# Hard-max attention on one core: dots grouped by four tiles, three GpSimd drains in the loop, and a reordered serial tail

## The chip, the core and the metric

The kernel runs on one core of one Trainium2 chip. The metric is the device time of one execution in microseconds (us); lower is better. A profile of one execution accompanies each kernel. Engines are named as in the profile: PE (TensorE matmul), PEld (its weight loads), DVE (VectorE), ACT (ScalarE), POOL (GpSimd), SP (the queue of SyncE).

## The reference

```python
B, Sq, Sk, D = 4, 4096, 4096, 128        # q, k, v: float32
logits = np.matmul(q, k.transpose(0, 2, 1))
best = np.argmax(logits, axis=-1)
return v[b_idx, best, :]                 # one row of v for each query
```

No softmax and no weighted sum: only the winning key's value row is needed.

## The kernel before

The queries are cut into 128 tiles of 128 rows. For each tile:

1. PE scores groups of four keys, with sums and differences of keys; ACT evicts with Abs or Relu, DVE folds what is left (`W`) and takes the eight highest groups with one MAX8 (`TOP`).
2. GpSimd gathers, by an indirect DMA per tile, the three key differences of the best group (`kg`). DVE computes three dots per row with them (product, two halvings, a reduction), and `pick` selects the winner within the group.
3. GpSimd gathers the value rows (`vr`), one indirect DMA per tile, and SP stores them.
4. Rows whose winner is in doubt are collected. The second half's are rechecked in a serial tail: gathers `FR`, `FQ`, three `FK`, exact dots, a last value gather `FV`, and a scatter into the output. A branch (`all_rows`) guards a fallback over everything.

The program order on each engine is fixed by a small scheduler that runs when the kernel is built. An iteration `it` places the instructions of a tile; the key gathers wait in `near_q`, the value gathers in `late_q`, and `issue` hands out a few of each per iteration:

```python
def dots(c, x, m):
    ...
    # start 2 iterations (1 in the last 24) after the key gathers are issued
    yield "until", lambda: ("kg", x) in done, 1 if x >= TAIL else 2
    nc.vector.tensor_tensor(out=prod, in0=kg, in1=..., op=OP.mult)          # m = 2 tiles
    yield "dve",
    nc.vector.tensor_tensor(out=p1, in0=prod[..., 0:64], in1=prod[..., 64:128], op=OP.add)
    yield "dve",
    nc.vector.tensor_tensor(out=p2, in0=p1[..., 0:32], in1=p1[..., 32:64], op=OP.add)
    yield "dve",
    nc.vector.tensor_reduce(out=d[:, x - c0:x - c0 + m, 1:4], in_=p2, ...)

def issue(it):
    ...
    while near_q and (n < 1 + (it >= T - 28 and len(near_q) > 2) or near_q[0] in marks):
        g = near_q.pop(0)
        n += g not in marks
        g()
    ...
    take_late(2 if n == 0 and len(late_q) > 4 or it >= T - 24 and it % 2 == 0 else 1)

def flags_last(...):                      # the serial tail, cut
    late(LATE)                            # 8 value gathers
    get(FR, ...); get(FQ, ...); late(1)
    ...
    get(FK[:, 0:3], ...)                  # three gathers
    late(3)
    win = whole(exact(FK, FQ, gb, 3, "fe"))
    get(FV, v_flat, win, B * Sk)
    late(1 << 20)
    ...
    all_rows()                            # loads the count of hard rows, branches
    nc.gpsimd.indirect_dma_start(out=out_flat, ..., in_=FV, ...)
```

A `mark` stands in `near_q` behind the gathers of a group; when it is popped, the group's dots get their place.

## Time and profile before

| | |
|---|---|
| median of the runs | 466.7 us (466.5 to 467.3) |
| span of the profiled execution | 465.5 us, mean granted PE clock 0.949 |
| last MAX8 starts | 420.1 us; 45.5 us of serial tail follow |
| final GpSimd drain | 454.19 to 464.68 us |

The page's first part gives busy time, share of the span and instructions of each engine. Its second part gives the busy tenths of an engine in 40 equal slices of the span. Of the kernel before:

```profile
PE 380.2 (82%) x1834; PEld 168.3 (36%) x1834; DVE 417.8 (90%) x825; ACT 376.8 (81%) x437; POOL 318.1 (68%) x345
...
DVE  2689999999999999999999999999998999998330
...
POOL 8233557877677888776678876677777777767730
```

DVE looks like the limit and POOL, with 68%, like an engine with room. Here is POOL's timeline of the kernel before, in the middle of the span (start, duration, engine, line, operation, output and input; in brackets the idle time before it and what ended that):

```profile
197.14 1.01 POOL L304 DMA_INDIRECT vr<-in_v_dram,win  x1 [0.30 <-issue]
198.45 0.95 POOL L250 DMA_INDIRECT kg<-k,cand  x1 [0.30 <-issue]
199.70 1.01 POOL L304 DMA_INDIRECT vr<-in_v_dram,win  x1 [0.30 <-issue]
201.01 0.94 POOL L250 DMA_INDIRECT kg<-k,cand  x1 [0.30 <-issue]
...
206.39 0.94 POOL L250 DMA_INDIRECT kg<-k,cand  x1 [0.57 <-DVE p L269]
```

Each gather occupies POOL for about 1.0 us and is followed by 0.30 us in which POOL is idle but waits for nothing ("issue"). A gather therefore costs 1.25 to 1.31 us of POOL's time.

The tail, in POOL's timeline of the kernel before, and the drains of the program's last line:

```profile
444.37 1.00 POOL L304 DMA_INDIRECT vr<-in_v_dram,win  x1 [0.30 <-issue]
447.55 1.00 POOL L498 DMA_INDIRECT FV<-in_v_dram,xw_fe  x1 [2.19 <-DVE hi L573]
454.42 1.03 POOL L534 DMA_INDIRECT out_dram<-FV,rowk_e  x1 [5.87 <-issue]
```

```profile
L806 POOLq DRAIN  x3: 46/109/10489, 454.2 to 465.2; - x3
```

The second fence is the view of one source line: the least, median and greatest duration in ns of three records. The long drain is placed ahead of the scatter's own time because POOL's sequencer reaches it while the scatter is still queued: it ends at 464.68 us, 9.2 us after the scatter's issue ended (455.45).

### The profile page before, as it was taken

Reading aid. Unit: us, or ns where it says so; the run is one execution under the profiler, and the core shown is the slowest. Engines: PE = TensorE matmul, PEld = TensorE weight load, DVE = VectorE, ACT = ScalarE, POOL = GpSimd, SP = SyncE. Lnnn points to the kernel's source line nnn. Section 1 sums busy time; section 2 is a strip of 40 time slices with the busy share of each in tenths; the row PEclk is TensorE's granted clock in tenths of the full one; section 3 lists DMA queues with packets and bytes.
Section 4 is the critical chain, followed back from the end, with each engine's and each line's share of the span. In section 5 each row is a group of like instructions: output and inputs, shape, how many; then the busy total and the mean of one; then the engine's idle time right before and its main releaser. Section 6 shows DMA issues by size and latency. Waiting matters only on the chain.

```text
span 465.5 us, 6396 instructions
## 1 busy us (share of the span) xinstructions
PE 380.2 (82%) x1834; PEld 168.3 (36%) x1834; DVE 417.8 (90%) x825; ACT 376.8 (81%) x437; POOL 318.1 (68%) x345
## 2 busy tenths in 40 slices
PE   8999999998999889999998889998998888850100
PEld 4444444443444344444443334443333333320000
DVE  2689999999999999999999999999998999998330
ACT  2999999999999989999997889999998888840000
POOL 8233557877677888776678876677777777767730
PEclk9999999999999999999999999999999999995555
DMA  7934576853325877943235653423432333322320
GB/s 130 227 66 96 107 103 97 139 120 85 80 76 135 148 140 128 121 126 81 79 98 137 129 116 94 100 80 87 110 101 79 86 86 99 87 71 68 94 74 4
DMA packets 43624, 47.54 MB, mean 102 GB/s; under 512 B 25000, under 2 KB 33451, under 8 KB 43584
## 3 DMA queue, kind: packets, MB, share of 16 engines
q0 software_dynamic: 18752, 30.97, 33.7%
q1 hardware_dynamic: 24832, 16.13, 13.1%
q8 instruction: 14, 0.23, 0.2%
q14 instruction: 26, 0.21, 0.2%
HBM read 39.59 MB, written 12.19 MB: 111 GB/s over the span
## 4 chain that ended last, share of the span: by engine, by line
DVE 31%; issue 23%; ACT 13%; PE 13%; DMA 9%; POOL 7%; POOLq 0%; DVEq 0%; ACTq 0%
DVE W L228 14%; ACT A L202 10%; PE psn L193 5%; DVE TOP L232 5%; PE psn L212 4%; DMA kg<-k,cand 4%; ACT E L215 4%; DMA vr<-in_v_dram,win 3%; DVE prod L265 3%; PE pd L193 3%; POOL kg L250 3%; POOL vr L304 2%; DVE D L274 2%; DVE p L269 2%; DMA natk<-in_k_dram 2%
## 5 line engine op out<-in xcount | busy, mean ns | idle before, releaser
L202 ACT ACTIVATE A<-pd 128x1024 f16<-128x1024 f32 x256 | 258.6, 1041 | 23.0 <-PE pd L193 22.7
L250 POOL DMA_INDIRECT kg<-k,cand x128 | 127.4, 995 | 85.1 <-issue 26.6
L228 DVE SCALAR_TENSOR_TENSOR W<-psn,E 128x1024 int16<-128x1024 f32 x128 | 166.0, 1297 | 7.0 <-ACT E L215 5.5
L193 PE MATMUL pd<-kT,qT 128*128 128x512 f16 x512 | 151.8, 378 | 15.7 <-ACT A L202 14.8
L193 PE MATMUL psn<-kT,qT 128*128 128x512 f16 x512 | 151.8, 378 | 15.3 <-ACT A L202 7.9
L304 POOL DMA_INDIRECT vr<-in_v_dram,win x128 | 136.6, 1067 | 39.0 <-issue 37.5
L193 PEld LDWEIGHTS <-qT 128*128 128x128 f16 x1024 | 98.4, 97 | 163.9 <-issue 76.0
L232 DVE MAX8 TOP<-W 128x8 f32<-128x1024 f32 x128 | 155.8, 1217 | 0.0
L212 PE MATMUL psn<-A,identh 128*128 128x512 f16 x512 | 152.1, 378 | 0.0
L215 ACT ACTIVATE E<-psn 128x1024 int16<-128x1024 f32 x128 | 132.2, 1033 | 5.0 <-PE psn L212 5.0
L212 PEld LDWEIGHTS <-identh 128*128 128x128 f16 x512 | 49.6, 97 | 60.8
L265 DVE TENSOR_TENSOR prod<-kg,natq 128x768 f16<-128x768 f16 x64 | 34.9, 546 | 3.9 <-DMA kg<-k,cand 3.9
L269 DVE TENSOR_TENSOR p<-prod 128x384 f16<-128x384 f16 x64 | 22.3, 349 | 0.1
L274 DVE TENSOR_REDUCE D<-p 128x6 f32<-128x192 f16 x64 | 21.5, 336 | 0.1
L173 ACT ACTIVATE kT<-uk 128x256 f16<-128x256 f32 x48 | 20.1, 419 | 0.9 <-PE uk L170 0.9
L64 POOL DMA_DIRECT2D natk<-in_k_dram x27 | 16.1, 599 | 0.9 <-POOLq L795 0.8
L67 POOL DMA_DIRECT2D natq<-in_q_dram x27 | 16.3, 605 | 0.2
L169 PE MATMUL uk<-identh,natk 128*128 128x128 f16 x96 | 15.8, 218 | 0.6 <-ACT A L202 0.6
L272 DVE TENSOR_TENSOR p<-p 128x192 f16<-128x192 f16 x64 | 15.7, 245 | 0.0
L464 PE MATMUL fp_e<-n_e,tri 128*128 128x1 f32 x2 | 0.6, 361 | 16.7 <-DVE n_e L462 16.7
L170 PEld LDWEIGHTS <-natk 128*128 128x128 f16 x96 | 9.3, 97 | 7.7 <-issue 5.3
L169 PEld LDWEIGHTS <-natk 128*128 128x128 f16 x96 | 9.3, 97 | 5.6
(147 smaller groups left out, 133.5 us busy)
## 6 DMA issues: line engine op xcount, KB each, us to landing
out_dram<-vr SPq DMA_DIRECT2D x32, 256.0 KB, 2.2
natq<-in_q_dram POOLq DMA_DIRECT2D x26, 128.0 KB, 3.2
k<-kd SPq DMA_DIRECT2D x8, 384.0 KB, 4.2
natk<-in_k_dram POOLq DMA_DIRECT2D x24, 128.0 KB, 3.9
kg<-k,cand POOLq DMA_INDIRECT x128, 2.8
vr<-in_v_dram,win POOLq DMA_INDIRECT x128, 2.8
natq<-in_q_dram POOLq DMA_DIRECT2D x1, 768.0 KB
natk<-in_k_dram POOLq DMA_DIRECT2D x1, 512.0 KB, 5.2
```

What stands on the lines that cost most here:

```text
L169: nc.tensor.matmul(out=o, lhsT=natk[b % 2][:, h, 4 * m + x, :], rhs=identh, start=True, stop=False)
L193: nc.tensor.matmul(out=ps[:, n * 512:(n + 1) * 512], lhsT=qT[b % 2][:, qt * P:(qt + 1) * P], rhs=kT[b % 2][:, u * 1024 + n * 512:u * 1024 ...
L202: nc.scalar.activation(out=A, in_=ps, func=AF.Abs)
L212: nc.tensor.matmul(out=ps[:, n * 512:(n + 1) * 512], lhsT=identh, rhs=A[:, n * 512:(n + 1) * 512], start=False, stop=True)
L215: nc.scalar.activation(out=E, in_=ps, func=AF.Relu, scale=QSCALE)
L228: nc.vector.scalar_tensor_tensor(out=W_t[t % NW].bitcast(I16)[:, 1::2], in0=ps, scalar=QSCALE, in1=E, op0=OP.mult, op1=OP.max)
L232: nc.vector.max(out=TOP[:, t, :], in_=W_t[t % NW].bitcast(FP32))
L250: near_q.append(lambda j=j: nc.gpsimd.indirect_dma_start(out=kg[:, j].rearrange("p f d -> p (f d)"), out_offset=None, in_=k16[t0 // NQT], ...
L265: nc.vector.tensor_tensor(out=prod, in0=kg, in1=natq[b % 2][:, x - b * NQT:x - b * NQT + m, :].unsqueeze(2).to_broadcast([P, m, 3, P]), op ...
L269: nc.vector.tensor_tensor(out=p1, in0=prod[:, :, :, 0:64], in1=prod[:, :, :, 64:128], op=OP.add)
L274: nc.vector.tensor_reduce(out=d[:, x - c0:x - c0 + m, 1:4], in_=p2, axis=AX_X, op=OP.add)
L304: late_q.append(lambda j=j: nc.gpsimd.indirect_dma_start(out=vr[:, j, :], out_offset=None, in_=v_flat, in_offset=IOA(ap=win[:, i + j:i + j ...
```

## The change

Its intent: pay for the long final drain in pieces inside the loop; take FV's landing out of the branch's wait; shorten the last dependent steps; and save DVE's fixed cost per operation by dots over four tiles up to tile 72. The diff, cut to its core:

```diff
+DRAINS = (28, 60, 92)
-LATE = 8
+LATE = 7
@@ dots
-        yield "until", lambda: ("kg", x) in done, 1 if x >= TAIL else 2
+        yield "until", lambda: ("kg", x) in done, 2 if m < 4 and x < TAIL else 1
+        # product in halves of two tiles; p1, p2 and the reduction over all m tiles;
+        # for m = 4 these are spread over several iterations
@@ flags_last
-        late(3)
-        win = whole(exact(FK, FQ, gb, 3, "fe"))
-        get(FV, v_flat, win, B * Sk)
         late(1 << 20)
         ...
-        all_rows()
+        win = whole(exact(FK, FQ, gb, 3, "fe"))
+        all_rows(hi)
+        get(FV, v_flat, win, B * Sk)
@@ issue
-        while near_q and (n < 1 + (it >= T - 28 and len(near_q) > 2) or near_q[0] in marks):
+        if it in DRAINS:
+            nc.gpsimd.drain()
+            owed[0] += 2
+            return
+        behind = len(near_q) > (2 if it >= T - 28 else 4)
+        while near_q and (n < 1 + behind or near_q[0] in marks):
...
+        # two owed value gathers are caught up, one every third iteration
@@ gathers
+            m = 4 if t1 <= T - 56 else 2 if t < T - 2 else 1
@@ after the loop: cand and key gather of tile T-2 ahead of fold(T-1); flags_first ahead of the last two dots
```

More of the change, by code (lines that the diff above doesn't have):

```diff
@@ L21 @@
 QSCALE = 128.0
+DRAINS = (28, 60, 92)
 TAU = 8.0
 NEAR = 0.5
-LATE = 8
+LATE = 7
+NKG = 6
 @with_exitstack
@@ L245, in gather @@
                                 op0=OP.bitwise_and, op1=OP.bitwise_xor)
-        kg = rp.tile([P, n, 3, P], FP16, tag=f"kg{n}", name=f"kg_{t0}", bufs=8)
-        assert len(kg_t) < 8
+        kg = rp.tile([P, 4, 3, P], FP16, tag="kg", name=f"kg_{t0}", bufs=NKG)[:, 0:n]
+        assert len(kg_t) < NKG
         kg_t[t0] = kg
@@ L261, in dots @@
         b = x // NQT
-        yield "until", lambda: ("kg", x) in done, 1 if x >= TAIL else 2
+        gap = ("wait", 1) if m == 4 else ("dve",)
+        yield "until", lambda: ("kg", x) in done, 2 if m < 4 and x < TAIL else 1
         kg = kg_t.pop(x)
-        prod = rp.tile([P, m, 3, P], FP16, tag=f"prod{m}", name=f"prod_{x}")
-        nc.vector.tensor_tensor(out=prod, in0=kg, in1=natq[b % 2][:, x - b * NQT:x - b * NQT + m, :].unsqueeze(2).to_broadcast([P, m, 3, P]),
-                                op=OP.mult)
-        yield "dve",
-        p1 = rp.tile([P, m, 3, 64], FP16, tag=f"p1{m}", name=f"p1_{x}")
+        prod = rp.tile([P, 4, 3, P], FP16, tag="prod", name=f"prod_{x}")[:, 0:m]
+        h = min(m, 2)
+        for i in range(0, m, h):
+            nc.vector.tensor_tensor(out=prod[:, i:i + h], in0=kg[:, i:i + h],
+                                    in1=natq[b % 2][:, x + i - b * NQT:x + i + h - b * NQT, :].unsqueeze(2).to_broadcast([P, h, 3, P]),
+                                    op=OP.mult)
+            yield gap
+        p1 = rp.tile([P, 4, 3, 64], FP16, tag="p1", name=f"p1_{x}")[:, 0:m]
         nc.vector.tensor_tensor(out=p1, in0=prod[:, :, :, 0:64], in1=prod[:, :, :, 64:128], op=OP.add)
-        yield "dve",
-        p2 = rp.tile([P, m, 3, 32], FP16, tag=f"p2{m}", name=f"p2_{x}")
+        yield gap
+        p2 = rp.tile([P, 4, 3, 32], FP16, tag="p2", name=f"p2_{x}")[:, 0:m]
         nc.vector.tensor_tensor(out=p2, in0=p1[:, :, :, 0:32], in1=p1[:, :, :, 32:64], op=OP.add)
@@ L274, in dots @@
         nc.vector.tensor_reduce(out=d[:, x - c0:x - c0 + m, 1:4], in_=p2, axis=AX_X, op=OP.add)
-        done.add(("dot", x))
+        done.update(("dot", i) for i in range(x, x + m))
     def pick(c, t0, t1):
@@ L280, in pick @@
         d = D_t[c % 4][:, 0:n, :]
-        yield "until", lambda: all(("dot", x) in done for x in range(t0, t1, 2)), 0
+        yield "until", lambda: all(("dot", x) in done for x in range(t0, t1)), 0
         cand = cand_t.pop(c)
@@ L524, in flags_last @@
             nc.vector.tensor_tensor(out=HARD, in0=HARD, in1=a, op=OP.add)
-        late(3)
-        win = whole(exact(FK, FQ, gb, 3, "fe"))
-        get(FV, v_flat, win, B * Sk)
         late(1 << 20)
+        hi = fp.tile([1, 1], mybir.dt.int32, tag="hi")
+        nc.vector.tensor_copy(out=hi, in_=HARD[0:1, :])
         ok = fp.tile([P, 1], FP32, tag="ok", name="ok_e")
@@ L557, in exact @@
         yield "dve", 0.17
-        win = fp.tile([P, 1], U32, tag="xw", name=f"xw_{name}")
+        win = fp.tile([P, 1], U32, tag=f"xw{R}", name=f"xw_{name}")
         nc.vector.tensor_reduce(out=win, in_=lt, axis=AX_X, op=OP.min)
@@ L569, in whole, with all_rows @@
                 return s.value
-    def all_rows():
-        hi = fp.tile([1, 1], mybir.dt.int32, tag="hi")
-        nc.vector.tensor_copy(out=hi, in_=HARD[0:1, :])
+    def all_rows(hi):
         left = nc.values_load(hi[0:1, 0:1], min_val=0, max_val=1 << 24,
@@ L679, in issue @@
             rest[0] = it + 3
-        take_late(2 if n == 0 and len(late_q) > 4 or it >= T - 24 and it % 2 == 0 else 1)
+        more = n == 0 and len(late_q) > 4 or it >= T - 24 and it % 2 == 0
+        if owed[0] and n < 2 and it % 3 == 0 and len(late_q) > 2:
+            owed[0] -= 1
+            more = True
+        take_late(2 if more else 1)
+    owed = [0]
     def gathers(t):
         for c, (t0, t1) in enumerate(chunks):
-            if t0 <= t < t1 and ((t - t0) % 2 or t == t1 - 1):
-                x = t0 + (t - t0) // 2 * 2
-                gather(c, x, t - x + 1)
+            m = 4 if t1 <= T - 56 else 2 if t < T - 2 else 1
+            if t0 <= t < t1 and (t - t0) % m == m - 1:
+                gather(c, t - m + 1, m)
             if t == t0:
@@ L747 @@
     top(T - 2)
+    gathers(T - 2)
+    flush()
     fold(T - 1)
     top(T - 1)
-    gathers(T - 2)
     gathers(T - 1)
@@ L771 @@
         dot = [s for s in live if s["kind"] == "dots" and s["c"] == c]
+        last = c == len(chunks) - 1
         while dot:
-            two, dot = dot[:2], dot[2:]
+            if last and len(dot) == 2:
+                flags_first(T // 2, T)
+            two, dot = (dot[:1], dot[1:]) if last else (dot[:2], dot[2:])
             drain(two)
-        last = c == len(chunks) - 1
-        if last:
-            flags_first(T // 2, T)
         drain([p], "cnt" if last else None)
```

## The prediction

> **What bounds it now.** One tile takes about 2.93 us in the middle of the span. In the timeline the VectorE starts there follow one another without a gap: start to start, fold W 1.19, MAX8 1.14, and for a pair of tiles product 0.47, two halvings 0.27 and 0.16, reduction 0.25, candidate 0.06: 5.87 us for two tiles. VectorE is busy 20.0 of 20.0 us in the windows from 40 to 100 us. ScalarE is nearly as full (19.5 to 20.0; three evictions of 0.92 start to start, plus a 0.37 us key copy in two of three tiles). The loop ends near 421 us; 44 us of serial tail follow. Its last part, in the records of the L576, L534 and L806 lines: the branch on the hard-row count is loaded at 447.6, waits for the last value gather FV to land (450.7), clears semaphores for 2.4 us, and the last scatter starts at 454.42. Then a GpSimd drain runs until 464.68, about 9.2 us after the scatter's issue ended, though the scatter landed near 456.7.
>
> **Change, piece by piece.**
> 1. Drains. GpSimd issued 324 DMAs. I take the final drain's length to grow with the DMAs since the previous drain (inferred from the edit; one long drain doesn't show it). About 85 remain after the drain in iteration 92: an estimate is 9.2 x 85/324 = 2.4 us instead of 9.2; with the scatter's landing as floor, I take 6 us off. Each drain in the loop costs GpSimd 2 to 3 us; GpSimd is 68% busy and waits for VectorE there, so most is hidden; up to 1 us of late gathers.
> 2. Branch ahead of FV. The wait for FV's landing (3.1 us after its start) leaves the branch, which now waits for an earlier gather; the chain becomes branch, FV, scatter. About 1 to 2 us.
> 3. Single-tile last gathers, tile 126's key gather before the last fold, flags ahead of the last dots. Now the last key gather starts at 423.09 and its product at 425.92. One gather (1.3 us) less in front, a shorter last dot, and 0.7 us of flag work moved ahead: 2.5 us earlier. The recheck read FR stands behind 7 value gathers instead of 8 (1.3 us each), so GpSimd passes the gain on. Together with 2: about 5 us.
> 4. Dots of four tiles for tiles 0 to 71. The product stays split in pairs, so per four tiles it saves one start each of two halvings, the reduction and the candidate: 0.05 to 0.07 us fixed part each (from 0.27 at 384 against 0.16 at 192 elements), 0.24 us, 4.3 us over 18 groups. The Trainium skill, "VectorE: DVE Perf Modes", rules for kernel authors, says to minimise the op count; the trace's fixed parts agree. But ScalarE has hardly any slack before 100 us and needs about 23.6 us for 8 tiles later against VectorE's 23.9, so only 1.5 us reaches the time.
>
> **Sum.** 6 + 5 + 1.5 - 0.5 = 12 us: 454.5 us, 8 in 10 between 450.5 and 460. Faster by over 2%: 0.74; within 2%: 0.24; slower: 0.02.
>
> **What would show it.** The last drain under 4 us; three drains of 2 to 3 us in the loop with VectorE gapless beside them; last TOP 1 to 2 us earlier; FV after the branch.
>
> **What would make it wrong.** A drain of fixed length: no gain at the end and 9 us of stalled gathers at three places. Gathers that lag after a drain, so products wait for kg. The 2.4 us clear being longer ahead of FV. ScalarE setting the pace throughout, so four-tile dots give nothing.

## The result, and the profile after

| | before | after |
|---|---|---|
| median | 466.67 us (466.47 to 467.32, 4 runs) | 477.97 us (477.23 to 478.18, 4 runs) |
| span of the profiled execution | 465.5 us | 476.4 us |
| last MAX8 starts | 420.1 us | 435.4 us |
| from there to the end | 45.5 us | 41.0 us |

The ratio is 1.0237 (95% interval 1.0219 to 1.0255): slower by 2.4%. A ratio here is the mean time of one kernel's fast runs over that of the other's of the same rounds, so it is not quite the ratio of the quoted medians.

The tail became 4.5 us shorter; the loop became 15.3 us longer. The lines of the page and of the waits (engine and line, what it waited for, us in total, times, longest) after the change:

```profile
PE 383.7 (81%) x1834; PEld 168.9 (35%) x1834; DVE 415.3 (87%) x758; ACT 377.3 (79%) x437; POOL 317.6 (67%) x345
...
DVE  2689999999999988899999999988985999889730
...
POOL 9313458747778887747778876377777777676740
```

```profile
POOL kg L252 <- issue: 48.5, 97, 7.3
...
DVE prod L270 <- DMA kg<-k,cand: 20.3, 16, 3.1
```

DVE has less work (415.3 us instead of 417.8), and no longer runs gapless. It waited 20.3 us in 16 places for key gathers; before, the same two waits were

```profile
POOL kg L250 <- issue: 26.6, 86, 0.8
...
DVE prod L265 <- DMA kg<-k,cand: 3.9, 3, 1.8
```

The drains, by the view of their source lines (three in the loop, then those of the program's end), and POOL's and DVE's timelines around the second:

```profile
L679 POOLq DRAIN  x3: 9603/10947/12037, 94.5 to 299.9; - x3
```

```profile
L823 POOLq DRAIN  x3: 46/109/10321, 465.2 to 476.1; - x3
```

```profile
199.46 1.31 POOL L252 DMA_INDIRECT kg<-k,cand  x1 [0.30 <-issue]
208.08 0.95 POOL L252 DMA_INDIRECT kg<-k,cand  x1 [7.31 <-issue]
```

```profile
209.20 1.29 DVE L230 SCALAR_TENSOR_TENSOR W<-psn,E 128x1024 int16<-128x1024 f32 x1
211.59 0.56 DVE L270 TENSOR_TENSOR prod<-kg,natq 128x768 f16<-128x768 f16 x1 [1.10 <-DMA kg<-k,cand]
```

A drain's record starts when POOL's sequencer reaches it, with about four gathers still queued in front of it on the engine. So 12.04 us of record are 6.6 us of standstill after the last gather's issue, and 7.31 us from gather to gather. And the final drain hardly got shorter: it still ends 9.05 us after the scatter's issue. The end of the tail after the change, in POOL's timeline, with FV behind the branch:

```profile
462.62 0.99 POOL L504 DMA_INDIRECT FV<-in_v_dram,xw_fe  x1 [5.10 <-DMA out_dram<-vr]
465.49 1.03 POOL L541 DMA_INDIRECT out_dram<-FV,rowk_e  x1 [1.87 <-DMA FV<-in_v_dram,xw_fe]
```

### The profile page after: what moved, and what is told of

Read it like the earlier page. It is cut to its first block, busy times and chain, and to the rows that moved or that the text cites. A ratio compares the mean times of both kernels' runs of the same rounds, so it can differ in the third digit from the quotient of the medians.

```text
span 476.4 us, 6325 instructions
## 1 busy us (share of the span) xinstructions
PE 383.7 (81%) x1834; PEld 168.9 (35%) x1834; DVE 415.3 (87%) x758; ACT 377.3 (79%) x437; POOL 317.6 (67%) x345
## 5 line engine op out<-in xcount | busy, mean ns | idle before, releaser
L310 POOL DMA_INDIRECT vr<-in_v_dram,win x128 | 134.3, 1049 | 39.0 <-issue 37.2
L270 DVE TENSOR_TENSOR prod<-kg,natq 128x768 f16<-128x768 f16 (+1 forms) x65 | 35.4, 545 | 20.4 <-DMA kg<-k,cand 20.3
L275 DVE TENSOR_TENSOR p<-prod 128x384 f16<-128x384 f16 (+2 forms) x47 | 19.9, 423 | 0.1
L280 DVE TENSOR_REDUCE D<-p 128x6 f32<-128x192 f16 (+2 forms) x47 | 19.3, 413 | 0.1
L278 DVE TENSOR_TENSOR p<-p 128x192 f16<-128x192 f16 (+2 forms) x47 | 13.5, 288 | 0.1
```

The lines of the kernel that those rows point to most:

```text
L270: nc.vector.tensor_tensor(out=prod[:, i:i + h], in0=kg[:, i:i + h], in1=natq[b % 2][:, x + i - b * NQT:x + i + h - b * NQT, :].unsqueeze(2 ...
L275: nc.vector.tensor_tensor(out=p1, in0=prod[:, :, :, 0:64], in1=prod[:, :, :, 64:128], op=OP.add)
L310: late_q.append(lambda j=j: nc.gpsimd.indirect_dma_start(out=vr[:, j, :], out_offset=None, in_=v_flat, in_offset=IOA(ap=win[:, i + j:i + j ...
```

## The experiments

### What the runs can be used for

The eighteen runs went out in seven jobs. Three of the jobs (ten runs) fell on chips where the kernel before itself took 502 to 520 us, at a mean granted clock of 0.915 to 0.936 instead of 0.945 to 0.950; in the traces of the kernels that ran beside it the clock fell to one half again and again, and the kernels' differences there mix with that. Their ratios are not used. On an undisturbed chip, the kernel before took 465 to 470 us. All main readings below are from four jobs (eight runs); the disturbed ones stand together at the end of this section. All differences between kernels below are near or under 2%; where one is called a gain or a loss, that rests on the interval of its ratio.

### How long a drain takes

For each long drain I took from POOL's records the time from the end of the last DMA issue before it to its end, and counted the DMAs issued since the previous drain (or since the program's start):

| kernel | DMAs since the last drain | us from the last issue's end |
|---|---|---|
| after, drains 1 to 3 | 61, 80, 73 | 5.06, 6.60, 6.03 |
| before with drains, 1 to 3 | 64, 78, 70 | 5.30, 6.44, 5.78 |
| after, final | 110 | 9.05 |
| before with drains, final | 112 | 9.21 |
| before, final | 324 | 9.23 |
| after without drains, final | 324 | 9.23 |

Eight drains lie on a straight line of 0.082 to 0.083 us a DMA (5.06/61, 9.21/112). The two over 324 DMAs don't: they have the length of about 112. (In the run with the look-up restored, below, 113 DMAs gave 9.29 us.) So both readings that I had held against each other were half right: the length does grow with the DMAs since the last drain, but not all the way. I call this a cap near 112; no count between 113 and 324 was measured, so whether the length stays the same in between or starts over once is not shown. The kernel before paid at its end for 112 DMAs, and not for its 324. The changed kernel pays for 61 + 80 + 73 = 214 more inside the loop, 17.7 us of POOL's time, and for 110 at the end, which saves 0.2 us.

### The drains alone, on the kernel before

```diff
 # kernel before, in issue()
+        if it in DRAINS:              # (28, 60, 92)
+            nc.gpsimd.drain()
+            owed[0] += 2
+            return
 # and the two owed value gathers, as in the change
```

> The kernel before with the three drains and their skipped iterations alone. Theory A: a drain costs GpSimd about 0.083 us for each DMA issued since the last one, at most about 112 of them (the four drains of the changed kernel, from the end of the last issue to the drain's end: 5.06, 6.60, 6.03 and 9.05 us after 61, 80, 73 and 110 DMAs; before, 9.23 after 324). So 5 to 7 us of stall each, 8 to 15 us slower than before in all, 475 to 482 us, and still about 9 us of drain at the end. Rival B: within 2 us of before.

Measured: 468.31 us against 467.00, ratio 1.0035 (1.0007 to 1.0063). The drains were as long as expected, 5.3 to 6.4 us, and yet the program lost only some 1.6 us. The expected 8 to 15 us were a miss: the stalls are real, but here they were hidden. What hid them can be counted. In POOL's DMA records I summed the idle time beyond the usual 0.30 us between one issue and the next, leaving out the gap that holds a drain:

| POOL's spare time, us, by tile | 32 to 64 | 64 to 100 | 100 to 127 |
|---|---|---|---|
| before | 3.8 | 8.7 | 3.5 |
| before with drains | 0.0 | 0.9 | 0.3 |
| after without drains, look-up at each turn (below) | 1.9 | 5.6 | 1.7 |
| the same with drains | 0.0 | 0.6 | 0.5 |
| after without drains | 2.6 | 6.6 | 5.2 |
| after | 0.0 | 2.8 | 5.4 |

The kernel before had 16.0 us to spare from tile 32 on. From gather to gather the three drains took 6.1, 7.1 and 6.6 us, and used up 14.8 us of it. POOL at "68% busy" was full afterwards.

### The changed kernel without its drains

```diff
-DRAINS = (28, 60, 92)
+DRAINS = ()
```

> A repeat of the kernel without drains: the chip of the first job ran even the kernel before at 502 to 513 us, with dips of the granted clock. Theory A: on a chip where before takes 467 us, last MAX8 near 418 us, tail near 41 us, 459 to 461 us; VectorE's wait for kg under 5 us. Rival B (four-tile dots make VectorE wait for kg): near 475.

Measured: 468.25 us against 467.00, ratio 1.0030 (1.0004 to 1.0055). The drains, with the iterations that they skip, account for 9.7 of the changed kernel's 11.3 us (477.97 - 468.25, in different jobs). But the rest of the change, from which I had expected a gain of 6 us, was no gain either. The loop was ahead of the kernel before by 4.4 us at tile 80 (MAX8 of that tile at 265.0 instead of 269.4), and then took 85.2 us from tile 104 to tile 127, where the kernel before took 76.9. The tail was 41.0 us, as in the changed kernel. DVE's waits, and its timeline where the loss begins:

```profile
DVE prod L270 <- DMA kg<-k,cand: 11.9, 6, 3.5
```

```profile
346.86 0.25 DVE L278 TENSOR_TENSOR p<-p 128x192 f16<-128x192 f16 x1
349.61 0.56 DVE L270 TENSOR_TENSOR prod<-kg,natq 128x768 f16<-128x768 f16 x1 [2.49 <-DMA kg<-k,cand]
...
352.93 0.24 DVE L278 TENSOR_TENSOR p<-p 128x192 f16<-128x192 f16 x1
356.68 0.56 DVE L270 TENSOR_TENSOR prod<-kg,natq 128x768 f16<-128x768 f16 x1 [3.51 <-DMA kg<-k,cand]
```

The order of the DMAs on POOL shows why (k a key gather, v a value gather, F one of the recheck's DMAs; the last 64 of POOL's DMAs):

```
before               vkvvkvkvvkvkvvkvkvvkFvkvkvkFvvkvkkvkvvkvkkvkkkvvvvvvvvFFvFFFvvFF
after, no drains     kvvvkkvvvkkvvvkkvvvkkvvvkkFvvvkkFvvkkvvkkvvkkvkkvvvvvvvFFvFFFvFF
```

In the changed program the two key gathers of a pair go out together. This comes from the line of the diff that looks like a mere rewriting: `behind` is computed once, ahead of the loop. In the kernel before the condition was looked up at each turn. With two gathers and a mark in `near_q` its length is 3, one gather is popped, the length is 2, and the loop stops; the second gather goes out in the next iteration. With the look-up made once, both go out at once, the mark follows in the same iteration, and the pair's dots are placed one iteration earlier. DVE then reaches the product before POOL has got to the gather, behind three value gathers in a row. The line also acts in the stage of the four-tile dots, where the limit is 4: four gathers and a mark make five, and two go out at once. In the traces of the kernels without drains, with the look-up made once and at each turn, the order of POOL's DMAs differs from the start.

### That look-up alone, in both directions

```diff
 # kernel before
-        while near_q and (n < 1 + (it >= T - 28 and len(near_q) > 2) or near_q[0] in marks):
+        behind = it >= T - 28 and len(near_q) > 2
+        while near_q and (n < 1 + behind or near_q[0] in marks):
```

> A repeat on another chip: the kernel before, with the look-up whether GpSimd is behind made once ahead of the issue loop. Theory D: 6 to 9 us slower than before, last MAX8 near 427 us instead of 420, all of it after tile 100. Rival: within 1 us of before.

Measured: 472.90 us against 466.95, ratio 1.0129 (1.0111 to 1.0147): 6 us slower by this line alone, with the last MAX8 at 425.8. The tail did not become shorter here: 46.7 us against 45.5. (The profiled execution had lost 1.2 us before tile 100 already, with a 3.4 us dip of the clock at 256 us; the rest came after.) DVE's waits for key gathers were

```profile
DVE prod L265 <- DMA kg<-k,cand: 8.4, 5, 2.5
```

And the other way round, the changed kernel without drains, with the look-up at each turn:

```diff
 # changed kernel, DRAINS = ()
-        behind = len(near_q) > (2 if it >= T - 28 else 4)
-        while near_q and (n < 1 + behind or near_q[0] in marks):
+        limit = 2 if it >= T - 28 else 4
+        while near_q and (n < 1 + (len(near_q) > limit) or near_q[0] in marks):
```

> A repeat on another chip: the last job's chip ran even the kernel before at 508 to 520 us with many dips of the granted clock, and its ratios are not used. The changed kernel without drains, with the look-up whether GpSimd is behind made at each turn. Theory D: against 468.3 without drains alone, 459 to 462 us; VectorE's wait for kg under 5 us. Rival: 468.

Measured: 463.73 us against 466.95, ratio 0.9929 (0.9911 to 0.9946). The 4.5 us between this and the run without drains (in different jobs) are the look-up's; the wait was

```profile
DVE prod L270 <- DMA kg<-k,cand: 5.1, 3, 2.9
```

It is short of the expected 459 to 462 us, because the tail grew from 41.0 to 44.3 us: with the gathers going out one by one the last dots and picks come later, and three value gathers instead of one stand between the last FK and the branch, which waits for them to land. The look-up made once had cost 6.8 us in the loop (last MAX8 at 425.6 against 418.8; 1.9 us of it by tile 80, 265.0 against 263.1) and had given back 3.3 us in the tail.

### Does restoring either one hide the drains again?

Why did the drains cost 9.7 us here and 1.6 us there? One theory (E) was the grace: the four-tile dots start one iteration after their gathers instead of two.

```diff
 # changed kernel, with its drains
-        ..., 2 if m < 4 and x < TAIL else 1
+        ..., 2 if x < TAIL else 1
```

> Second repeat: the changed kernel with its drains, a four-tile dot starts two iterations after its last key gather's issue. Theory E: 472 to 475 us, and the 5.9 us that the first two drains cost up to tile 92 shrink to under 2. Rival (GpSimd is short of time in all): 477 to 478.

Measured: 477.18 us against 466.83, ratio 1.0216 (1.0157 to 1.0274), so the rival's number. The first drain's cost did go (MAX8 of tile 48 3.1 us ahead of before, as without drains), the second's did not (tile 68 1.0 us behind, without drains 3.3 ahead). Theory E falls as the main cause. The waits only moved:

```profile
DVE prod L270 <- DMA kg<-k,cand: 17.1, 14, 4.0
```

The other was the look-up, with the drains kept:

> Second repeat: the changed kernel with its drains, the look-up at each turn as before. Theory D: the loss between tiles 92 and 127 (12.5 us against before) shrinks to 4 to 6, 470 to 472 us. If GpSimd is short of time in all: 474 to 476.

(The edit is the one above, with DRAINS as in the change.) Measured: 473.81 us against 466.83, ratio 1.0147 (1.0087 to 1.0206). About 4 us came back (from 477.97, in different jobs), the look-up's own cost, the lower end of what had been expected if POOL is short of time in all. Against the same kernel without drains the ratios give 1.0147/0.9929 = 1.022: there the drains cost 2.2%, 10 us, to some 3 us by the two intervals (the two profiled executions are 8.0 us apart), so about as much look-up or not. The table of spare time fits this only in part. Here the faster loop left POOL 9.2 us instead of 16.0, drains of about 20 us used 8.1 of it, and an estimate from these is a loss of 12 us; for the kernel before the same sum is 20 - 15 = 5, where 1.6 was measured. For the changed kernel itself it is 20 - 6 = 14, where 9.7 was measured. So the sum is 1.5 to 4 us too high. And it can be made only afterwards: the changed kernel without drains had 14.4 us to spare, nearly as much as the kernel before, but its drains used up only 6.2 of it. That POOL stands still for the drains and that DVE then waits for its gathers is shown; why the kernel before could hide so much more of this stays open.

### What the rest of the change is worth

Tail changes alone: no drains, look-up at each turn, and two-tile dots (with `NKG` back at 8 buffers for key gathers, as many as before).

```diff
 # changed kernel without drains, look-up at each turn
-            m = 4 if t1 <= T - 56 else 2 if t < T - 2 else 1
+            m = 2 if t < T - 2 else 1
```

> The changed kernel without drains, look-up at each turn, dots of two tiles throughout: the tail's changes alone. If GpSimd sets the pace from tile 32 on, the four-tile dots' lead is taken back and this comes within 1.5 us of the 463.7 us of no_drains_rule_b: 464 to 465.5 us, last MAX8 near 420, tail 44 to 44.5. Rival (the four-tile dots carry the gain): 466 to 467.

Measured: 465.97 us against 466.72, ratio 0.9984 (0.9955 to 1.0014), the same as before within its interval; the tail was 44.2 us instead of 45.5. With four-tile dots the ratio was 0.9929, so these are worth about 0.5%, 2.5 us, with intervals that nearly touch. In the two profiled executions their lead over two-tile dots was 5.3 us at tile 80 (MAX8 at 263.1 against 268.4) and 0.4 us at the last tile (418.8 against 419.1). The rest of these two loops, from tile 80 to the last MAX8, four-tile dots first (busy us of PE, PEld, DVE, ACT and POOL with the instructions, then the granted clock, the DMA share and GB/s):

```profile
263.10:418.80 155.70, 128.75 (x570) 53.58 (x568) 150.56 (x318) 128.60 (x140) 115.84 (x114) 0.99 0.34 93
268.40:419.10 150.70, 127.62 (x566) 53.37 (x565) 147.79 (x305) 127.59 (x139) 109.70 (x108) 0.99 0.33 92
```

DVE was busy there 2.8 us longer with the four-tile dots: more than half of the lead at tile 80 was work put off (dots of 74 tiles had been begun by then, against 76). The rest went into waits for key gathers, 4.2 us against 1.7 after tile 80.

### A version that beats both

In the changed kernel the pairs shorten the tail when they come at the very end, and the hope was that they cost little if they come only there:

```diff
 # changed kernel without drains
+        limit = 2 if it >= T - 28 else 4
+        pair = it >= 120 and len(near_q) > limit
+        while near_q and (n < 1 + (pair or len(near_q) > limit) or near_q[0] in marks):
```

> No drains, look-up at each turn up to iteration 119, pairs of key gathers together from 120 on, so that only one value gather instead of three stands between the last recheck gather and the branch. Tail 41 us as in no_drains_b instead of 44.3, at 1 to 3 us of waits in the last 8 tiles: 461 to 463.5 us. If the waits are worth more than the shorter tail: 464 to 466.

Measured: 462.00 us against 466.72, ratio 0.9899 (0.9869 to 0.9928): the lowest median of all kernels here, 1.0% faster than before. (Its interval overlaps that of the look-up at each turn throughout, 0.9911 to 0.9946.) POOL's timeline of its tail has one value gather ahead of the branch, the scatter is issued at 448.52, and the waits for key gathers are small:

```profile
438.26 1.00 POOL L504 DMA_INDIRECT FK<-in_k_dram,gb_e  x1 [0.31 <-issue]
439.56 1.10 POOL L310 DMA_INDIRECT vr<-in_v_dram,win  x1 [0.30 <-issue]
445.76 0.99 POOL L504 DMA_INDIRECT FV<-in_v_dram,xw_fe  x1 [5.10 <-DMA out_dram<-vr]
448.52 1.03 POOL L541 DMA_INDIRECT out_dram<-FV,rowk_e  x1 [1.76 <-DMA FV<-in_v_dram,xw_fe]
```

```profile
DVE prod L270 <- DMA kg<-k,cand: 3.4, 4, 1.2
```

The tail was 41.5 us. Its last 9 us are still the final drain.

### The runs on disturbed chips

These ten gave correct results. First job (before: 502 to 513 us): the changed kernel without drains 511.5 (ratio 1.0088), with the drains taken out but their iterations still skipped 516.8 (1.0176), the four-tile dots alone 513.5 (1.0141), the tail alone 505.1 (0.9934).

> The changed kernel without its three drains, all else kept. Theory A (the drains stop GpSimd for 5 to 7 us each, and VectorE then waits for late key gathers): the loss goes, last MAX8 near 418 us instead of 435.4, the tail stays near 41 us, total about 459 to 461 us; VectorE's wait for kg falls from 20.3 us to under 5; the final drain stays at about 9 us after the last scatter. Rival B (four-tile dots, with one iteration of grace instead of two, make VectorE wait for kg): the wait stays near 20 us and the total near 475.

> The changed kernel with the drain instructions taken out, but the three iterations still skip their gathers and the two owed gathers are caught up. Theory A: as without drains, within 1 us, 459 to 462 us. Rival C (the skipped iteration and the backlog it leaves is what costs): near 475 us, as with drains.

> Only the four-tile dots up to tile 72 (with their issue rule and buffers); tail as before, no drains. Prediction on record: 1.5 us faster than the kernel before (465.2). If the changed kernel's early lead (last MAX8 of tile 32 was 2.2 us ahead of before's when no drain had yet stopped it) lasts: 463 to 465. Rival B: slower than before by several us.

> Only the tail's changes (branch ahead of FV, single-tile last gathers, flags earlier, seven late gathers); dots of two tiles throughout, no drains. The changed kernel's tail from its last MAX8 to the end was 41.0 us against 45.5: so about 4.4 us faster than before, 462 us; if the sum holds, no_drains = this plus quad_only.

Second such job (before: 508 to 520 us): the look-up on the kernel before 525.6 (1.0302), no drains with look-up at each turn 531.9 (1.0394), the changed kernel with look-up at each turn 548.5 (1.0728), with a grace of two 536.3 (1.0531).

> The kernel before, with one thing of the change: whether GpSimd is behind is looked up once ahead of the issue loop instead of at each turn, so in the last 28 iterations both key gathers of a pair go out in one iteration and the dots that read them are placed one iteration earlier. Theory D (this is what costs at tiles 104 to 127: VectorE waits for kg there[...]): 6 to 9 us slower than before, 473 to 476 us, last MAX8 near 427 instead of 420, no change before tile 100. Rival: the four-tile dots' backlog costs there: within 1 us of before.

> The changed kernel without drains, and with the look-up made at each turn as before. Theory D: the 8 us lost between tiles 104 and 127 come back, 459 to 462 us, VectorE's wait for kg under 5 us. Rival (four-tile dots or late gathers cost there): near 468 as without the drains.

> The changed kernel with its drains, only the look-up at each turn as before. Theory D: 5 to 9 us of the changed kernel's loss come back, 469 to 473 us; the part that the drains cost together with the four-tile dots stays.

> The changed kernel with its drains, only that a four-tile dot starts two iterations after its last key gather's issue, as a two-tile dot does, instead of one. Theory E (a drain delays gathers by 5 to 7 us; the kernel before hides that, since its dots stand two iterations behind the gathers, the four-tile dots with one iteration don't): VectorE's waits for kg between 160 and 225 us go (6.5 us in five waits), 471 to 474 us. Rival: GpSimd is short of time in all, the waits only move, 477.

Third (before: 507 to 520 us): grace of two 543.2 (1.0661), look-up at each turn 548.6 (1.0736).

> Repeat on another chip of: the changed kernel with its drains, a four-tile dot starts two iterations after its last key gather's issue instead of one. Theory E (the grace hid the drains in the kernel before): the 5.9 us that the first two drains cost up to tile 92 shrink to under 2, 472 to 475 us. Rival (GpSimd is short of time in all): the waits only move, 477 to 478.

> Repeat on another chip of: the changed kernel with its drains, the look-up at each turn as before. Theory D: the loss between tiles 92 and 127 (12.5 us against before) shrinks to 4 to 6, 470 to 472 us. If GpSimd is short of time in all, a backlog is left to the tail instead and less comes back, 474 to 476.

What they do show is the clock. In the first job's run without drains, in two neighbouring windows (busy us of PE, PEld, DVE, ACT and POOL with the instructions, then the granted clock, the DMA share and GB/s):

```profile
85.00:100.00 15.00, 14.77 (x73) 6.68 (x72) 15.00 (x23) 15.00 (x19) 12.23 (x13) 1.00 0.62 119
100.00:115.00 15.00, 11.13 (x50) 4.57 (x48) 10.82 (x14) 9.90 (x12) 11.34 (x13) 0.98 0.38 105
```

PE, DVE and ACT all fall idle together, PE with gaps that the profile ends with "issue", ahead of the dip of the clock at 114.3 us. What stops PE on these chips and not on the others stays open. So does what the skipped iterations alone cost (the second run listed, 516.8 beside 511.5 us, with intervals that overlap).

## Why the prediction was wrong

It said 454.5 us; 478.0 was measured. Of these 23.5 us the drains hold 15: 5.5 were forecast as their gain, 9.7 measured as their loss.

1. **Drains: the step that failed, twice.** "I take the final drain's length to grow with the DMAs since the previous drain": it does, at 0.083 us each, up to 113 of them, but the 324 of the kernel before took no longer than 112. "About 85 remain": it was 110. So instead of 6 us off the end it was 0.2. And "GpSimd is 68% busy and waits for VectorE there, so most is hidden; up to 1 us of late gathers": the busy share leaves out the 0.30 us after each gather. From tile 32 on POOL had 16.0 us to spare in the kernel before, where the drains cost 1.6 us, and 14.4 in the changed kernel without them, where they cost 9.7: three times 5.8 to 7.3 us of standstill after an issue, and DVE's waits for key gathers rose from 11.9 us without drains to 20.3. The length of a drain in the loop, "2 to 3 us", was 5.1 to 6.6.
2. **A step that was missing.** The diff's `behind` line changes the order on POOL, in the stage of the four-tile dots and in the last 28 iterations. The prediction didn't mention it. It cost 6.0 us when put alone into the kernel before (where it acts in the last 28 only), and 4.5 us net here.
3. **Branch ahead of FV and the last gathers, about 5 us: right in sum, by luck.** The tail went from 45.5 to 41.0 us. But 3.3 of the 4.5 us came with the pairs of item 2; with the order restored the tail is 44.3 us, and these changes alone (two-tile dots) were worth 0.2%, within noise. The branch gained nothing by itself: from the last FK's start to the scatter's it was 12.7 us in the kernel before and 12.7 with the order restored, where three value gathers stand in front of it, and 10.4 with one. (The prediction's "clear" of 2.4 us is one INC_SWDGE_SEM instruction in the traces: 2.41 us before, and 2.35 ahead of FV.) The predicted step "2.5 us earlier" for the last dots was not seen as such: they ended 7.4 us after the last MAX8's start instead of 7.7. What shortened the changed kernel's tail were the seventh instead of eighth gather ahead of FR (13.2 us after the last MAX8 instead of 15.2), and the branch that no longer waits for FV (scatter at 30.1 us instead of 34.4).
4. **Four-tile dots, 1.5 us: about right in size at the end** (about 2.5 us, by ratios from two jobs), mostly for a different reason. The saving was nearly as summed (4.3 us): up to the last MAX8 DVE was busy for 396.2 us instead of 400.7 with two-tile dots. But what held it back was less ScalarE, whose evictions DVE waited for 3.2 instead of 2.0 us from 20 us on, than the key gathers, 5.1 instead of 1.7 us.

The prediction's list of what would make it wrong named "gathers that lag after a drain, so products wait for kg", and no gain at the end. That is what the runs show, with waits of 20.3 us and 0.2 us at the end; the error was to give it little weight.

## What to carry to other kernels

Before adding work to an engine with "room", count its room from its timeline: idle time beyond the gap that each of its instructions always has, stage by stage, and against the loop as fast as the change will make it. That is an upper limit and not a promise: of 14.4 us the drains could use 6.2. Before paying for a long final step in instalments, find out whether its length has an upper limit; where it has one, instalments can add up to more than the sum. In a kernel whose order is fixed when it is built, compare the order of instructions on each engine for every line of a diff, also for those that look like a rewriting: one condition evaluated once instead of at each turn was worth more than the saved operations.

## What the Trainium skill lacked or had wrong

- **A GpSimd drain's length** (no page has it). It was 0.082 to 0.083 us for each DMA that GpSimd issued since the last drain, up to 113 of them; 9.23 us after 324, and nothing measured between. A drain with no DMA since the last took 0.05 to 0.11 us. "GPSIMD Engine Reference", section 4, says that two of GpSimd's cores generate the descriptors of each such DMA; it gives no cost for draining them.
- **Drains at the program's end.** "VectorE: DVE Perf Modes", section "The DRAIN you can't avoid", describes those that the runtime adds as about 12 ns each, constant, on all five engines. The drains at the end of this program carry a line of kernel.py, so it is not shown that they are of that kind, and the page is not contradicted. On SP and DVE they were 7 to 17 ns, on ACT up to 81, but GpSimd's first at the end took 10.3 to 10.6 us in every undisturbed run; the page doesn't speak of a drain behind DMAs.
- **The gap between gathers.** No page that I found has it: a gather of one row per partition kept GpSimd busy for 1.0 us and was followed by 0.30 us of "issue", 123 times for the value gathers of the kernel before alone. With it, a busy share of 68% left 16.0 us to spare from tile 32 on.
- **The clock gate.** "TensorE: Matmul & The Clock Gate", part 1, says that the clock is gated to one half after an idle window of about 3.4 us (3413 ns), in a free-running window. The runs agree on size and step: the dips before the tail lasted 3.4, 6.8, 10.2, 13.7 or 17.1 us and were to one half. They don't show an idle window ahead of each: the dip of 6.8 us at 359.1 us in the undisturbed run without drains came right after DVE's two waits of 2.49 and 3.51 us, but in the 3.41 us before it PE, with its weight loads, was busy for 1.33 us, with no gap over 1.76 us. Not stated there: in three jobs, each on a chip of its own, the kernel before took 502 to 520 us instead of 467, at a mean clock of 0.915 to 0.936; what starts this stays open.
- One of the kernel before's 7 runs in one job took 1013.1 us at a granted clock of 1.0; it counts as slow and enters no ratio. No page and no run here explains it.
